# A hybrid layer on one core: who adds, gates and scales in the last round

## The chip, the core and the metric

The kernel runs on one core of one Trainium2 chip. The metric is the device time of one execution in microseconds (us). Before the change it is 2850.22 us, the median of 3 runs (2848.17 to 2852.48).

## What is computed

One layer of a hybrid network over a sequence of 2048 tokens of width 1024: a modulated norm, retention in both directions, grouped attention with a context of 256 tokens, an output projection, and then the part that matters here:

```python
x = x + g1 * (jnp.concatenate([ret, att], axis=-1) @ w_out)
h2 = _modulate(_rmsnorm(x, norm2_g), sh2, sc2)
x = x + g2 * _sqrelu_mlp(h2, w_ff1, w_ff2)      # square(relu(h2 @ w_ff1)) @ w_ff2, 4096 wide
...
return _rmsnorm(x, final_norm_g)                # x * rsqrt(mean(x*x) + eps) * g
```

The change concerns the last two lines: the residual sum with the gate `g2`, and the final norm, for the last of four slices of the hidden width.

## The kernel before

Products of the feed-forward part are made in split float16 (each float32 operand as a high and a low half, three matmuls for one product), and by a scheme with seven block products in place of eight. The second matmul is done in four rounds over the hidden width (`rd` 0 to 3). In a round the sixteen token tiles of 128 are taken in eight pairs, `PAIRS`, so there are 32 pairs in all, numbered 0 to 31; pairs 24 to 31 are the last round. A pair holds two token tiles, `g` = 0 and 1, and each tile has two halves of 512 columns, `n` = 0 and 1.

For each pair TensorE makes seven products (`down`, L1996 to L1998, 84 matmuls). `down_out` drains product `i` from PSUM: product 0 is copied by ScalarE (L2013), the others are added by VectorE to what was known (L2008). Four of these results are finished blocks and go to `gate`:

- after product 1 the block (`g` 0, `n` 0), after product 4 (1, 0), after product 5 (1, 1), after product 6 (0, 1);
- each is multiplied by the gate row `g2` (L2036) and added to the residual tile `y` (L2038);
- in the rounds before the last one the tile is stored to scratch; in the last round ScalarE squares each half and sums it (L2048), VectorE adds the two sums (L2056), GpSimd makes the root of the mean in two small ops (L1280, L1281), and VectorE multiplies the tile by the root and by the norm's weight in one op (L2063), after which it is stored.

GpSimd also makes the operands of the pair after (`sum_u`, L1981, four sums of 128x512 a pair); ScalarE rounds them to float16 (`hi_u`, L1985), and VectorE makes the remainder (`lo_u`, L1989, seven a pair).

Before the change all multiplications with the gate are on GpSimd, the sums for the halves `n` = 0 on GpSimd, and those for the halves `n` = 1 on VectorE. In the last pair both ops for the halves `n` = 1 are on VectorE.

The order on every engine is written out by hand: `on(at, phase, fn)` puts a call into a numbered step and a phase of it. Step by step, and in a step phase by phase, the calls are made in this order, and each engine runs its instructions in the order in which they were issued:

```python
FPHASES = ("pe", "sum", "hi", "lo", "relu", "out", "square", "late", "dma")
...
s = NU + 7 * p
...
on(s - 7, "sum", sum_u, p, "s1", "a21", "a22", ALU.add)
on(s - 6, "sum", sum_u, p, "s2", "s1", "a11", ALU.subtract)
on(s - 5, "sum", sum_u, p, "s3", "a11", "a21", ALU.subtract, "a21")
on(s - 3, "sum", sum_u, p, "s4", "a12", "s2", ALU.subtract, "s2")
```

So pair `p` begins at step `s`; a step is one product; the operand sums of a pair fall into the steps of the pair before. All transfers are issued from SyncE's queue (SP).

Of the kernel before, what the change touches and what calls it, by code (L numbers as in the profile page):

```python
# [11 lines left out]
F32 = mybir.dt.float32  # L12
F32R = mybir.dt.float32r
F16 = mybir.dt.float16
BF16 = mybir.dt.bfloat16
I32 = mybir.dt.int32
AF = mybir.ActivationFunctionType
ALU = mybir.AluOpType
# [4 lines left out]
P = 128  # L23
D = 1024
# [31 lines left out]
def layer_kernel(ctx: ExitStack, tc: tile.TileContext, a: dict, out: bass.AP):  # L56
    nc = tc.nc
# [27 lines left out]
    def scratch(name, n, shape, dtype=F32):  # L85
        return [dram.tile(shape, dtype, name=f"{name}{i}", tag=f"{name}{i}") for i in range(n)]
# [13 lines left out]
    x1_d = scratch("x1", NT, [P, D])  # L100
# [162 lines left out]
    with ExitStack() as st, tc.manual_schedule():  # L263
# [5 lines left out]
        op = st.enter_context(tc.tile_pool(name="op", bufs=2, reuse_waits="tile"))  # L269
        sm = st.enter_context(tc.tile_pool(name="sm", bufs=3, reuse_waits="tile"))  # L270
# [162 lines left out]
        class Rows:  # L433
# [11 lines left out]
            def square(self, n):  # L445
                if n % self.k == 0:
                    self.ss = sm.tile([P, self.k], F32, name="ss", tag=f"ss{self.k}", bufs=2)
                junk = tp.tile([P, D], BF16, name="junk", tag="junk", bufs=1)
                m = n % self.k
                nc.scalar.activation(junk, self.x[n], AF.Square, accum_out=self.ss[:, m : m + 1])  # L450
# [63 lines left out]
        g2 = one.tile([P, 2, 2, HD], F32, name="g2")  # L514
# [511 lines left out]
        for (g, c), w in weights.items():  # L1026
            if (g, c) > (0, 0):
                s = first[g, w.col]
# [5 lines left out]
        for g in (1, 2):  # L1034
            rows = Rows(GROUPS[g], 3)
            s = first[g - 1, C_RV]
# [33 lines left out]
        def slots(*what):  # L1070
            return [first[g, col] + n for g, col, ns in what for n in ns]

        two = (0, 0, 1, 1, 2, 2, 3, 3, 4, 4, 5, 5)
        at = slots((0, C_RQ, range(4)), (0, C_RV, two), (1, C_AQ, (1, 2, 3, 4)), (1, C_RK, (0, 0, 1, 2, 2, 3, 4, 4, 5)))
# [6 lines left out]
        at = slots((0, C_AKV, range(1, 6)), (0, C_AQ, range(4)), (0, C_RQ, range(4)), (1, C_AQ, range(6)))  # L1081
# [8 lines left out]
        s = first[2, C_RG]  # L1090
# [3 lines left out]
        for i in range(NK):  # L1094
            at = min(s + i + 1, len(units) - 1)
# [102 lines left out]
        for s, (g, c, m) in enumerate(units):  # L1198
# [3 lines left out]
            ps = psO.tile([P, 512], F32, name="pso", tag="pso")  # L1202
# [7 lines left out]
        s = len(units)  # L1210
# [9 lines left out]
    def pool(stack, name, bufs=1, **kw):  # L1220
        return stack.enter_context(tc.tile_pool(name=name, bufs=bufs, reuse_waits="tile", **kw))

    qp = pool(attn, "qp")
    op = pool(attn, "op2", 2)
# [4 lines left out]
    sm = pool(side, "sm2", 3, side="right")  # L1229
# [29 lines left out]
    def on(k, phase, fn, *args):  # L1259
        events.setdefault((k, phase), []).append((fn, args))  # L1260
# [16 lines left out]
    def rsqrt_chain(src, n, scale, tag, chain=chain, eps=EPS):  # L1277

        v, y = (sm.tile([P, n], F32, name=f"c{x}_{tag}", tag=f"c{x}_{tag}") for x in "vy")
        chain.append(lambda: nc.gpsimd.tensor_scalar(v, src, scale, eps, op0=ALU.mult, op1=ALU.add))  # L1280
        chain.append(lambda: nc.gpsimd.tensor_tensor(y, v, half[:, :n], op=ALU.pow))  # L1281
        return y
# [198 lines left out]
    def output_weights(k0):  # L1481
# [26 lines left out]
        for i in range(2 * KT):  # L1508
            k, n = i % KT, i // KT
            j = k0 + 4 + 4 * i  # L1510
            if i % 2 == 0:
                on(k0 + 1 if i == 0 else j - 5, "dma", fetch, k, n)
            on(j, "late", gate, k, n)
            on(j + 1, "late", part, k, n, 0)
            on(j + 2, "late", part, k, n, 1)
# [166 lines left out]
    ff = {}  # L1682
# [270 lines left out]
    PAIRS = [(rd, hf, q) for rd in range(4) for hf in range(2) for q in range(4)]  # L1953
    NAMES = ("a11", "a12", "a21", "a22")
    FORMS2 = ("a11", "a12", "s2", "s3", "a22", "s1", "s4")
    w2, uf, raw2, ys = {}, {}, {}, {}
# [14 lines left out]
    def tiles_of(p):  # L1971
        _, hf, q = PAIRS[p]
        return halves[hf][q], halves[hf][q + 4]
# [26 lines left out]
    xs_ = {}  # L2000

    def down_out(at, p, i):

        ps = pu.pop(i)

        def add(x, to=None):
            to = to if to is not None else ff["r"].tile([P, 512], F32, "d")
            nc.vector.tensor_tensor(to, ps, xs_[x], op=ALU.add)  # L2008
            return to

        if i == 0:
            xs_["x"] = ff["r"].tile([P, 512], F32, "d")
            nc.scalar.activation(xs_["x"], ps, AF.Copy)  # L2013
        elif i == 1:
            gate(at, p, 0, 0, add("x"))
        elif i == 2:
            xs_["u2"] = add("x")
        elif i == 3:
            xs_["u3"] = add("u2")
        elif i == 4:  # L2020
            gate(at, p, 1, 0, add("u3"))
        elif i == 5:
            gate(at, p, 1, 1, add("u3", xs_["u3"]))
            add("u2", xs_["u2"])
        elif i == 6:
            gate(at, p, 0, 1, add("u2", xs_["u2"]))

    sums = {}

    def gate(at, p, g, n, c):  # L2030
        s = slice(n * 512, (n + 1) * 512)
        y = ys[p, g][:, s]
        final = PAIRS[p][0] == 3
        fast = p == len(PAIRS) - 1 and n == 1
        eng = nc.vector if fast else nc.gpsimd
        on(at + 1, "square", lambda: eng.tensor_tensor(c, c, ff["g2"][:, s], op=ALU.mult))  # L2036
        eng2 = nc.vector if n or fast else nc.gpsimd
        on(at + 2, "lo" if eng2 is nc.vector else "square", lambda: eng2.tensor_tensor(y, y, c, op=ALU.add))  # L2038
        if not final:
            if n == 1:  # L2040
                on(at + 4, "dma", lambda: nc.sync.dma_start(x1_d[tiles_of(p)[g]], ys.pop((p, g))))
            return

        def square():
            if n == 0:
                sums[p, g] = ff["sm"].tile([P, 2], F32, name="ss", tag=f"ss{g}")
            junk = ff["sm"].tile([P, 512], BF16, name="junk", tag="junk", bufs=1)
            nc.scalar.activation(junk, y, AF.Square, accum_out=sums[p, g][:, n : n + 1])  # L2048

        on(at + 3, "relu", square)  # L2050
        if n == 1:
            on(at + 4, "lo", ending, at + 4, p, g)

    def ending(at, p, g):
        ss, y, t = sums.pop((p, g)), ys.pop((p, g)), tiles_of(p)[g]
        nc.vector.tensor_tensor(ss[:, :1], ss[:, :1], ss[:, 1:], op=ALU.add)  # L2056
        steps = []
        r = rsqrt_chain(ss[:, :1], 1, 1.0 / D, "e", steps)
        for step in steps:
            on(at, "square", step)  # L2060

        def whole(c):
            nc.vector.scalar_tensor_tensor(y[:, c], y[:, c], r, ff["fg"][:, c], op0=ALU.mult, op1=ALU.mult)  # L2063

        def store(c):
            nc.sync.dma_start(out[0, t * P : (t + 1) * P, c], y[:, c])

        n = 2 if p == len(PAIRS) - 1 else 1
        for i in range(n):
            c = slice(i * D // n, (i + 1) * D // n)  # L2070
            on(at + 1, "lo", whole, c)
            on(at + 1 if n == 2 else at + 3, "dma" if n == 1 else "lo", store, c)

    def down_jobs():
        for i in range(7):
            on(NU + 1 + i // 2, "dma", fetch_w2, 1, i)
        for p, (rd, hf, q) in enumerate(PAIRS):
            s = NU + 7 * p
            for m, blk in enumerate((2, 3, 0, 1)):
                on(s - 11 + m // 2, "dma", fetch_u, p, blk)  # L2080
            for g in range(2):
                on(s - 3 + g, "dma", fetch_y, p, g)
# [4 lines that stand above are left out]
            for i in range(7):  # L2087
                on(s - 7 + i, "hi", hi_u, p, i)
                on(s - 6 + i, "lo", lo_u, p, i)
                on(s + i, "pe", down, p, i)  # L2090
                on(s + i, "out", down_out, s + i, p, i)
                if (hf, q) == (1, 3) and rd in (0, 1):
                    on(s + i + 1, "dma", fetch_w2, rd + 2, i)
# [79 lines left out]
```

## Time and profile before

| what | value |
|---|---|
| median of 3 runs | 2850.22 us (2848.17 to 2852.48) |
| profiled execution | 2851.53 us |
| its span, first to last instruction | 2849.7 us |
| mean granted TensorE clock | 0.984 |
| TensorE busy | 2675.7 us, 94% of the span |
| VectorE busy | 2184.7 us, 77% |
| GpSimd busy | 1932.0 us, 68% |
| ScalarE busy | 1466.6 us, 51% |
| last matmul begins | at 2829.26 us |

How to read the lines that follow. A row of the timeline has the start from the beginning of the span and the duration, both in us, then the engine (PE is TensorE, DVE VectorE, ACT ScalarE, POOL GpSimd, SP SyncE), the line of the kernel, the operation, output and inputs by the program's names, the shapes, and how many instructions were merged into the row. In brackets stands how long the engine sat idle before it, and what ended the wait. A duration contains the time for which an instruction had been started but was held up, so it can be longer than the work. `pd` is a product in PSUM, `d` a block on its way to the residual, `y` a residual tile, `g2b` the gate row, `ss` the sums of squares, `cv_e` and `cy_e` the steps of the root, `fgb` the weight of the final norm, `ur` and `us` operands and their sums, `uf` their float16 halves.

### The profile page before, as it was taken

How to read it: one execution, taken by the hardware profiler on the slowest of the kernel's cores; microseconds unless marked ns; L12 is line 12 of the kernel's file. 1: busy time of each engine (PE TensorE's matmuls, PEld its weight loads, DVE VectorE, ACT ScalarE, POOL GpSimd, SP SyncE). 2: the span in 40 equal slices, each digit the busy share in tenths (PEclk: the TensorE clock that was granted, in tenths of full speed). 3: DMA queues.
4: the chain of work that ended last, by engine and by line, in shares of the span. 5: the costliest groups of instructions: out<-in, count | busy, mean ns of one | idle time of the engine just before them, and what ended most of it. 6: DMA issues, size and time to landing. Idle time of an engine off the chain costs nothing.

```text
span 2849.7 us, 46102 instructions
## 1 busy us (share of the span) xinstructions
PE 2675.7 (94%) x16756; PEld 1602.6 (56%) x16756; DVE 2184.7 (77%) x3122; ACT 1466.6 (51%) x2443; POOL 1932.0 (68%) x1499
## 2 busy tenths in 40 slices
PE   6899999898789999899999989999999999999996
PEld 3778688676556666566666634444444444444443
DVE  3587847778988777777778549788886688888898
ACT  2443443334677777777777735555554322222232
POOL 2436517434766667887667659888875688888887
PEclk8999999999999999999999989999999999999998
DMA  6684975565511212444112354677784757575643
GB/s 211 217 301 158 313 262 165 176 217 169 190 32 62 87 51 71 119 113 112 51 62 69 143 179 145 191 244 244 246 277 129 256 174 273 172 276 170 196 141 111
DMA packets 330467, 482.82 MB, mean 169 GB/s; under 512 B 82807, under 2 KB 193655, under 8 KB 325758
## 3 DMA queue, kind: packets, MB, share of 16 engines
q1 hardware_dynamic: 329854, 479.60, 51.2%
q8 instruction: 132, 2.16, 0.3%
q14 instruction: 97, 0.79, 0.1%
q10 hardware_dynamic: 384, 0.26, 0.0%
HBM read 327.57 MB, written 152.20 MB: 168 GB/s over the span
## 4 chain that ended last, share of the span: by engine, by line
PE 56%; DVE 8%; POOL 5%; issue 3%; DMA 2%; ACT 1%; SPq 0%; POOLq 0%; DVEq 0%; ACTq 0%
PE pu L1780 7%; PE pu L1779 7%; PE pu L1781 7%; PE pd L1998 5%; PE pd L1996 5%; PE pd L1997 5%; PE o L239 3%; PE st L205 3%; PE st L206 3%; PE mp L168 2%; PE bank L1545 2%; PE bank L1546 2%; DVE plo L224 2%; DVE nm L181 2%; PE bank L1547 2%
## 5 line engine op out<-in xcount | busy, mean ns | idle before, releaser
L181 DVE TENSOR_REDUCE nm<-mp 128x1 f32<-128x512 f32 (+1 forms) x576 | 390.5, 684 | 165.9 <-PE mp L168 136.9
L222 POOL TENSOR_TENSOR plo<-p,phi 128x1024 f16<-128x1024 f32 x160 | 352.5, 2204 | 165.2 <-ACT phi L215 133.2
L211 ACT ACTIVATE p<-st 128x512 f32<-128x512 f32 x576 | 338.3, 597 | 201.0 <-PE st L206 117.8
L1779 PE MATMUL pu<-hf,w1f 128*128 128x512 f16 x896 | 340.9, 380 | 0.0
L1780 PE MATMUL pu<-hf,w1f 128*128 128x512 f16 x896 | 340.9, 380 | 0.0
L1998 PE MATMUL pd<-w,uf 128*128 128x512 f16 x896 | 339.6, 379 | 1.3 <-DVE uf L1989 1.2
L1781 PE MATMUL pu<-hf,w1f 128*128 128x512 f16 x896 | 340.7, 380 | 0.0
L1996 PE MATMUL pd<-w,uf 128*128 128x512 f16 x896 | 339.6, 379 | 0.0
L1997 PE MATMUL pd<-w,uf 128*128 128x512 f16 x896 | 339.6, 379 | 0.0
L215 ACT ACTIVATE phi<-p 128x1024 f16<-128x1024 f32 x288 | 303.9, 1055 | 0.0
L1012 PE MATMUL pso<-whi,hhi_l 128*128 128x512 f32 (+1 forms) x768 | 298.8, 389 | 0.7 <-ACT whi L508 0.7
L1014 PE MATMUL pso<-whi,hlo_l 128*128 128x512 f32 (+1 forms) x768 | 289.2, 377 | 10.3 <-DVE hlo_l L488 10.3
L1013 PE MATMUL pso<-wlo,hhi_l 128*128 128x512 f32 (+1 forms) x768 | 288.2, 375 | 1.4 <-DVE wlo L512 1.4
L238 PE MATMUL o<-wv,plo 128*128 128x65 f16 x2304 | 234.8, 193 | 27.3 <-POOL plo L222 18.1
L224 DVE TENSOR_TENSOR plo<-p,phi 128x512 f16<-128x512 f32 x256 | 244.3, 955 | 16.8 <-ACT phi L215 16.2
L2036 POOL TENSOR_TENSOR d<-d,g2b 128x512 f32<-128x512 f32 x126 | 199.8, 1586 | 68.6 <-DVE d L2008 65.6
L239 PE MATMUL o<-wv,phi 128*128 128x129 f16 x2304 | 242.6, 220 | 0.0
L238 PEld LDWEIGHTS <-plo 128*128 128x128 f16 x2304 | 205.7, 98 | 64.0 <-POOL plo L222 28.0
L1791 DVE TENSOR_TENSOR r<-pu,r 128x512 f32<-128x512 f32 x224 | 151.0, 686 | 114.5 <-PE pu L1781 96.0
L1796 POOL TENSOR_TENSOR r<-r 128x512 f32<-128x512 f32 x128 | 168.6, 1322 | 94.5 <-ACT r L1795 93.9
L205 PE MATMUL st<-qr,ks 128*128 128x512 f16 x576 | 219.3, 381 | 11.7 <-ACT p L211 9.9
L206 PE MATMUL st<-qr,ks 128*128 128x512 f16 x576 | 219.5, 381 | 0.1
(324 smaller groups left out, 6290.2 us busy)
## 6 DMA issues: line engine op xcount, KB each, us to landing
wm<-in_w_ff SPq DMA_DIRECT2D x64, 512.0 KB, 6.7
u<-r SPq DMA_DIRECT2D x128, 256.0 KB, 4.6
ur<-u SPq DMA_DIRECT2D x128, 256.0 KB, 4.9
y<-x SPq DMA_DIRECT2D x64, 512.0 KB, 6.2
wst<-in_w_in SPq DMA_DIRECT2D x60, 512.0 KB, 6.2
wf<-w2f SPq DMA_DIRECT2D x112, 256.0 KB, 3.7
w<-wf SPq DMA_DIRECT2D x28, 1024.0 KB, 8.7
w1r<-in_w_ff SPq DMA_DIRECT2D x48, 512.0 KB, 5.0
```

Of the source, the lines that this page charges most:

```text
L181: nc.vector.tensor_reduce(dst, src, axis=AX.X, op=ALU.max, negate=True)
L206: mm(ps, ks2[:, self.g, k], q[:, 1], start=False, stop=True)
L211: nc.scalar.activation(self.p[kt // 2][:, kt % 2], self.s.pop(kt), AF.Exp, scale=HD**-0.5)
L222: nc.gpsimd.tensor_tensor(lo, p, hi, op=ALU.subtract)
L238: mm(o[:, : HD + 1], lo[:, i, c], v[:, : HD + 1], start=False, stop=False)
L239: mm(o, hi[:, i, c], v[:, :VW], start=False, stop=last)
L1779: mm(pu[hf, i], whi, hi, start=k == 0, stop=False)
L1780: mm(pu[hf, i], whi, lo, start=False, stop=False)
L1781: mm(pu[hf, i], wlo, hi, start=False, stop=k == 3)
L1996: mm(ps, u[:, 0, b], w[:, b, 0], start=b == 0, stop=False)
L1997: mm(ps, u[:, 0, b], w[:, b, 1], start=False, stop=False)
L1998: mm(ps, u[:, 1, b], w[:, b, 0], start=False, stop=b == 3)
```

## The change

In the last round the sum for the half (`g` 0, `n` 1) moves from VectorE to GpSimd, in pairs 24 to 30; VectorE keeps that for (1, 1). In the last but one pair, 30, the final scaling of both tiles is done in two ops, on ScalarE (times the root) and on GpSimd (times the norm's weight), in place of one on VectorE. In the last pair, 31, the half `n` = 1 of each tile is gated in two parts: what is known before the last product is multiplied by the gate and added to the residual tile first (for tile 1 on GpSimd, for tile 0 on VectorE), and the last product itself is then multiplied by the gate straight from PSUM and added by VectorE.

```diff
         elif i == 4:
             gate(at, p, 1, 0, add("u3"))
+            if p == len(PAIRS) - 1:
+                on(at, "square", direct, p, 1, xs_["u3"], nc.gpsimd)
+        elif i == 5 and p == len(PAIRS) - 1:
+            direct(p, 1, ps, nc.vector)
+            add("u2", xs_["u2"])
+            direct(p, 0, xs_["u2"], nc.vector)
+            squares(at + 2, p, 1, 1)
+        elif i == 6 and p == len(PAIRS) - 1:
+            direct(p, 0, ps, nc.vector)
+            squares(at + 1, p, 0, 1)
...
+    def direct(p, g, src, eng):
+        y, t = ys[p, g][:, 512:], ff["r"].tile([P, 512], F32, "d")
+        eng.tensor_tensor(t, src, ff["g2"][:, 512:], op=ALU.mult)
+        eng.tensor_tensor(y, y, t, op=ALU.add)
+
+    def squares(at, p, g, n):
+        y = ys[p, g][:, n * 512 : (n + 1) * 512]
+
+        def square():
+            if (p, g) not in sums:
+                sums[p, g] = ff["sm"].tile([P, 2], F32, name="ss", tag=f"ss{g}")
+            junk = ff["sm"].tile([P, 512], BF16, name="junk", tag="junk", bufs=1)
+            nc.scalar.activation(junk, y, AF.Square, accum_out=sums[p, g][:, n : n + 1])
+
+        on(at, "relu", square)
+        if n == 1:
+            on(at + 1, "lo", ending, at + 1, p, g)
...
     def gate(at, p, g, n, c):
         s = slice(n * 512, (n + 1) * 512)
         y = ys[p, g][:, s]
         final = PAIRS[p][0] == 3
-        fast = p == len(PAIRS) - 1 and n == 1
-        eng = nc.vector if fast else nc.gpsimd
-        on(at + 1, "square", lambda: eng.tensor_tensor(c, c, ff["g2"][:, s], op=ALU.mult))
-        eng2 = nc.vector if n or fast else nc.gpsimd
-        on(at + 2, "lo" if eng2 is nc.vector else "square", lambda: eng2.tensor_tensor(y, y, c, op=ALU.add))
...
+        on(at + 1, "square", lambda: nc.gpsimd.tensor_tensor(c, c, ff["g2"][:, s], op=ALU.mult))
+        eng = nc.vector if n and (g or not final) else nc.gpsimd
+        on(at + 2, "lo" if eng is nc.vector else "square", lambda: eng.tensor_tensor(y, y, c, op=ALU.add))
+        if final:
+            squares(at + 3, p, g, n)
+        elif n == 1:
+            on(at + 4, "dma", lambda: nc.sync.dma_start(x1_d[tiles_of(p)[g]], ys.pop((p, g))))
...
     def ending(at, p, g):
...
+        def scaled():
+            nc.scalar.activation(y, y, AF.Copy, scale=r)
+
+        def weighted():
+            nc.gpsimd.tensor_tensor(y, y, ff["fg"], op=ALU.mult)
+
+        if p == len(PAIRS) - 2:
+            on(at + 1, "relu", scaled)
+            on(at + 1, "square", weighted)
+            on(at + 2, "dma", store, slice(0, D))
+            return
         n = 2 if p == len(PAIRS) - 1 else 1
```

More of the change, by code (lines that the diff above doesn't have):

```diff
@@ L2033, in gate @@
         final = PAIRS[p][0] == 3
-        fast = p == len(PAIRS) - 1 and n == 1
-        eng = nc.vector if fast else nc.gpsimd
-        on(at + 1, "square", lambda: eng.tensor_tensor(c, c, ff["g2"][:, s], op=ALU.mult))
-        eng2 = nc.vector if n or fast else nc.gpsimd
[L2038 to L2052, printed above, removed]
+        on(at + 1, "square", lambda: nc.gpsimd.tensor_tensor(c, c, ff["g2"][:, s], op=ALU.mult))
[5 more added lines that the diff above has]
+            on(at + 4, "dma", lambda: nc.sync.dma_start(x1_d[tiles_of(p)[g]], ys.pop((p, g))))
     def ending(at, p, g):
```

## The prediction, made before the changed kernel ran

> **What bounds the kernel now.** I began with the span and the chain of waits, went on to the timeline of ScalarE through the last round to get the pace of the pairs, then to one pair on GpSimd (POOL) and VectorE (DVE), and last to the twenty microseconds behind the last matmul.
>
> ```profile
> span 2849.7 us, 46102 instructions
> ```
> ```profile
> 2685.43 0.60 ACT L2013 ACTIVATE d<-pd 128x512 f32<-128x512 f32 x1 [4.55 <-PE pd L1998]
> 2703.56 0.60 ACT L2013 ACTIVATE d<-pd 128x512 f32<-128x512 f32 x1 [3.25 <-PE pd L1998]
> 2722.13 0.58 ACT L2013 ACTIVATE d<-pd 128x512 f32<-128x512 f32 x1
> ...
> 2825.66 0.58 ACT L2013 ACTIVATE d<-pd 128x512 f32<-128x512 f32 x1
> ```
>
> L2013 runs once in a pair and drains the pair's first product. Up to 2703.56 it waits for TensorE and comes every 18.13 us: that is TensorE's own pace. Then the wait is gone and the pairs come every 20.71 us (2722.13 to 2825.66 is 103.53, in five steps). So in the last round, whose pairs also carry the final norm, TensorE runs ahead and something slower sets the pace. One such pair on POOL, and DVE's part of it:
>
> ```profile
> 2800.85 1.65 POOL L2036 TENSOR_TENSOR d<-d,g2b 128x512 f32<-128x512 f32 x1 [1.76 <-DVE d L2008]
> 2802.58 1.72 POOL L2038 TENSOR_TENSOR y<-y,d 128x512 f32<-128x512 f32 x1
> 2804.26 1.72 POOL L2036 TENSOR_TENSOR d<-d,g2b 128x512 f32<-128x512 f32 x1
> 2805.94 1.26 POOL L1981 TENSOR_TENSOR us<-ur 128x512 f32<-128x512 f32 x1
> 2807.16 1.72 POOL L2036 TENSOR_TENSOR d<-d,g2b 128x512 f32<-128x512 f32 x1
> 2808.84 1.71 POOL L1981 TENSOR_TENSOR us<-us,ur 128x512 f32<-128x512 f32 x1
> 2810.51 1.71 POOL L1981 TENSOR_TENSOR ur<-ur 128x512 f32<-128x512 f32 x1
> 2812.20 1.72 POOL L2036 TENSOR_TENSOR d<-d,g2b 128x512 f32<-128x512 f32 x1
> 2814.01 0.19 POOL L1280 TENSOR_SCALAR cv_e<-ss 128x1 f32<-128x1 f32 x1
> ...
> 2818.11 1.67 POOL L1981 TENSOR_TENSOR us<-ur,us 128x512 f32<-128x512 f32 x1
> 2821.55 1.65 POOL L2036 TENSOR_TENSOR d<-d,g2b 128x512 f32<-128x512 f32 x1 [1.76 <-DVE d L2008]
> ```
> ```profile
> 2806.01 1.74 DVE L2038 TENSOR_TENSOR y<-y,d 128x512 f32<-128x512 f32 x1 [1.16 <-POOL d L2036]
> 2807.67 1.75 DVE L1989 TENSOR_TENSOR uf<-ur,uf 128x512 f16<-128x512 f32 x1
> 2809.35 1.75 DVE L2038 TENSOR_TENSOR y<-y,d 128x512 f32<-128x512 f32 x1
> 2811.02 0.68 DVE L2008 TENSOR_TENSOR d<-pd,d 128x512 f32<-128x512 f32 x1
> ...
> 2818.59 2.28 DVE L2063 SCALAR_TENSOR_TENSOR y<-y,cy_e,fgb 128x1024 f32<-128x1024 f32 x1
> ```
>
> Two things are to be seen. First, the two engines take turns. POOL's op at 2805.94 ends at 2807.20; DVE's add, begun at 2806.01, ends 0.55 us after that; POOL's next op, begun at 2807.16, takes 1.72. Left alone a POOL op advances its queue by 1.22 (2805.94 to 2807.16); with one DVE op between, by 1.68 (2807.16 to 2808.84). So a DVE op on two SBUF operands takes 0.46 of POOL's time, and a POOL op 1.22 of DVE's. DVE ops that read a product from PSUM (L2008) keep to 0.68 throughout. Second, POOL's 1.76 of idle time is a link of a loop, not slack. POOL runs without a break from 2800.85 to 2819.78; DVE's L2063, begun at 2818.59, gets through only after that (to 2820.87); the drain L2008 behind it feeds POOL's next product with the gate at 2821.55. The loop is POOL's run of 18.93 plus 1.77 for L2063 and the drain: 20.70, the pace of the pairs. A longer run means a slower pair.
>
> Now the end, behind the last matmul:
>
> ```profile
> 2829.26 0.38 PE L1998 MATMUL pd<-w,uf 128*128 128x512 f16 x1
> ```
> ```profile
> 2824.95 2.95 POOL L2036 TENSOR_TENSOR d<-d,g2b 128x512 f32<-128x512 f32 x2
> 2829.73 1.26 POOL L2036 TENSOR_TENSOR d<-d,g2b 128x512 f32<-128x512 f32 x1 [1.83 <-DVE ss L2056]
> 2831.08 0.19 POOL L1280 TENSOR_SCALAR cv_e<-ss 128x1 f32<-128x1 f32 x1
> 2831.35 0.55 POOL L1281 TENSOR_TENSOR cy_e<-cv_e,half 128x1 f32<-128x1 f32 x1
> ...
> 2836.89 1.27 POOL L2036 TENSOR_TENSOR d<-d,g2b 128x512 f32<-128x512 f32 x1 [2.00 <-DVE d L2008]
> ```
> ```profile
> 2826.70 2.35 DVE L2038 TENSOR_TENSOR y<-y,d 128x512 f32<-128x512 f32 x2 [1.16 <-POOL d L2036]
> ...
> 2831.94 2.27 DVE L2063 SCALAR_TENSOR_TENSOR y<-y,cy_e,fgb 128x1024 f32<-128x1024 f32 x1 [0.93 <-POOL cy_e L1281]
> ...
> 2834.93 1.28 DVE L2063 SCALAR_TENSOR_TENSOR y<-y,cy_e,fgb 128x1024 f32<-128x1024 f32 x1
> ...
> 2841.41 0.69 DVE L2038 TENSOR_TENSOR y<-y,d 128x512 f32<-128x512 f32 x1
> ```
>
> TensorE is done at 2829.64, and 20.06 us of elementwise work and stores remain. The last residual sum starts at 2841.41; from there to the end of the span (squares, root, scaling, stores of the last tile) are 8.29 us.
>
> **The change, part by part.** *The moved sum.* In pairs 24 to 30 the second half of the first tile's residual sum (DVE at 2809.35) goes to POOL; the built order puts it there between the operand sums that stood at 2808.84 and 2810.51. From 2804.26 to 2814.01 POOL now has six full ops, with five DVE turns between them: 6 x 1.22 + 5 x 0.46 = 9.62, and the rows say 9.75. Afterwards it has seven ops and four turns: 7 x 1.22 + 4 x 0.46 = 10.38. The run grows by 0.76 per pair. On DVE 1.67 goes (2809.35 to 2811.02), but DVE's queue waits for POOL at L2063 anyway. The square behind the moved sum comes later on ScalarE, and ahead of the two operand copies queued there; those wait for POOL's operand sum at 2810.51 in any case, so that costs nothing; without that cover it would be one square, 0.6. The bounds are 0 (the idle 1.76 is slack after all) and 1.22 a pair (DVE's freed turn is filled by another op of its own). I take 0.76, which is what the turns give. The loop sets the pace for the five steps from 2722.13; the first I count half, since ScalarE still waited 3.25 for TensorE at 2703.56: 4.5 x 0.76 = 3.4.
>
> *Pair 30 scaled elsewhere.* Two DVE ops (L2063, 2.27 and 1.28) become, for each tile, one ScalarE op on 128x1024 with the root as scale and one POOL product with the norm weight on 128x1024. The rows nearest:
>
> ```profile
> L215 ACT ACTIVATE phi<-p 128x1024 f16<-128x1024 f32 x288 | 303.9, 1055 | 0.0
> ```
> ```profile
> L222 POOL TENSOR_TENSOR plo<-p,phi x160: 2118/2132/2695, 674.1 to 1619.9; 128x1024 f16<-128x1024 f32 x160
> ```
>
> ScalarE: 1.06. POOL: two 128x512 advances make 2.44; below stands the median 2.13 of L222, whose output has half the bytes, above its 2.69 under contention. I take 2.44. [...] No row here has this form.
>
> *The last pair.* Its gate products and sums for the second halves are split: what is known goes first (on POOL for one tile, on DVE for the other), the last product is gated straight from PSUM. For the tile on POOL these two ops stand in the queue behind both 2.44 products, and DVE's sum of the same half waits for them. On the old clock, without the 3.4:
>
> - POOL ends the two gate products at 2827.90 and takes the moved sum behind DVE's one remaining sum (2828.36): 2829.6. The gate product of 2829.73 comes when it did, ends at 2830.8; root for one tile (2831.08 and 2831.35 above, 0.82 in all) to 2831.7; the sum, 1.22, to 2832.95. ScalarE scales meanwhile, to 2832.8.
> - First 2.44 product: 2835.4. Second root, 0.82: 2836.2. ScalarE's scaling, 1.06 and about 0.1 of handing over, with POOL standing behind it: 2837.4. Second product: 2839.85.
> - Only now the known part of the last pair: product and sum, 2 x 1.22: 2842.3. Before the change POOL's gate product of the last pair had begun at 2836.89.
> - POOL goes straight on with the other tile half's gate product, so DVE's sum gets in at 2843.5 and ends at 2844.1. POOL's sum follows to 2845.3 while DVE drains from PSUM (0.6); DVE's product with the gate gets in at 2845.3, to 2845.8; sum 0.6, product from PSUM 0.6; last sum at 2847.0.
>
> The last sum starts at 2847.0 instead of 2841.41: 5.6 later, with the same 8.29 behind it. If DVE wins the turn at 2842.3, its later ops lose theirs and the last sum comes at 2846.8. With 2.13 for the products it is 5.0, with 2.69 it is 6.1. The pair's two stores leave on SP behind POOL instead of DVE, at 2835.4 and 2839.85; with ten microseconds left they hide.
>
> *Sum:* 3.4 + 5.6 = 9.0. The profiled execution took 2851.53 (1.83 around its span), so it would take 2860.5; it stands 1.31 above the median of 2850.22, so the forecast is 2859.2.
>
> **The turns, once more.** The rows at 2805.94 to 2811.02 show an op that waits out the other's whole op. [...]
>
> **Rivals.**
> - *Only the tail* (0.10): the loop has slack, since DVE, a sum shorter, reaches L2063 earlier. 5.6, so 2855.8. Against it: L2063 already ends at POOL's release at 2819.78, not at its own start.
> - *Every freed turn is used* (0.09): 4.5 x 1.22 + 6.1 = 11.6, so 2861.8. For it: DVE has seven operand remainders (L1989) per pair, several undelayed now.
> - *DVE is the bound* (0.05), the other side: the idle 1.76 is true slack, and DVE's queue sets the pair. Then each pair loses DVE's 1.67, 4.5 x 1.67 = 7.5, and the tail loses the two L2063, 3.55: 2839.2. It decides from the point where POOL's added 1.22 fits into 1.76 without moving L2063. DVE's 1.16 wait for POOL at 2806.01 speaks against it.
> - *The late sums hide* (0.05): if the two 2.44 products don't hold up the last pair, only the 3.4 stays: 2853.6. It needs the last pair's sums to stand ahead of them in POOL's queue, and the built order has them behind.
>
> **Numbers.** The forecast, 2859.2, has 0.71 and a range of its own from 2856.5 to 2862. About 0.2%, 5.7 us, is what a measurement of this kernel can tell from no change. Slower by more: forecast, used turns, and half of the tail alone, 0.85. Same: the other half and the hidden sums, 0.10. Faster: 0.05. The range from 2854.5 to 2863 takes the bounds of the prices (5.0 with no loss in the loop, 6.1 with 1.22 a pair, and 1 of scatter at the top) and leaves out the DVE rival and the hidden sums.
>
> **What would show it.** Steps of 21.4 to 21.5 between L2013's rows from the second step on, and still an idle of about 1.8 before one gate product a pair, would show the loop; steps of 20.7 or less refute it. Two POOL products of 2.1 to 2.7 behind L2013's last row, POOL without a gap of over 1.3 up to the last pair's known sum, and DVE waiting for that sum by some 5 us would show the tail. Last matmul to end of span should grow from 20.1 to about 25.7. The forecast is wrong if DVE reaches its last residual sum as early behind the last L2013 as before, 15.75.

## The result, and the profile after

| | before | changed |
|---|---|---|
| median of 8 runs | 2849.51 us (2844.77 to 2853.1) | 2859.68 us (2854.62 to 2865.27) |
| ratio | 1 | 1.0038, 95% interval 1.0026 to 1.0049 |
| span of the profiled execution | 2849.7 us | 2861.6 us |
| step: from one pair's drain on ScalarE (L2013) to the next, last five | 20.71 us | 21.61 us |
| tail: from the last of these drains to the end of the span | 24.04 us | 29.83 us |
| from the last drain to the last residual sum on VectorE | 15.75 us | 21.52 us |

The changed kernel is 10.2 us slower by the medians; by the interval of the ratio the difference lies between 7.4 and 14 us. The forecast was 2859.2.

ScalarE's drains in the changed kernel, from its timeline (start, duration, in brackets the wait):

```profile
span 2861.6 us, 46105 instructions
```
```profile
2687.00 0.60 ACT L2013 ACTIVATE d<-pd 128x512 f32<-128x512 f32 x1 [4.55 <-PE pd L1998]
2705.13 0.60 ACT L2013 ACTIVATE d<-pd 128x512 f32<-128x512 f32 x1 [3.24 <-PE pd L1998]
2723.72 0.58 ACT L2013 ACTIVATE d<-pd 128x512 f32<-128x512 f32 x1
2745.33 0.58 ACT L2013 ACTIVATE d<-pd 128x512 f32<-128x512 f32 x1
...
2831.77 0.58 ACT L2013 ACTIVATE d<-pd 128x512 f32<-128x512 f32 x1
```

Up to the drain with the 3.24 wait nothing differs but a shift of 1.57 (2705.13 against 2703.56). It is there already at the first drain of the last round (2687.00 against 2685.43), ahead of every changed instruction. In the traces of all kernels of this document the drain that is at 2705.13 here comes between 2696.4 and 2705.1, so the shift is taken for scatter from one execution to the next; where it comes from is not shown. From that drain to the last are 126.64 us, against 122.10 before: 4.54 more. With the tail's 5.79 the change costs 10.33 in the traces; the medians say 10.17. In what follows step and tail are compared, not single times.

One pair on GpSimd, and two rows of VectorE from the same stretch:

```profile
2809.45 1.72 POOL L2062 TENSOR_TENSOR d<-d,g2b 128x512 f32<-128x512 f32 x1
2811.14 1.26 POOL L1981 TENSOR_TENSOR us<-ur 128x512 f32<-128x512 f32 x1
2812.36 1.72 POOL L2062 TENSOR_TENSOR d<-d,g2b 128x512 f32<-128x512 f32 x1
2814.04 1.72 POOL L1981 TENSOR_TENSOR us<-us,ur 128x512 f32<-128x512 f32 x1
2815.72 1.71 POOL L2064 TENSOR_TENSOR y<-y,d 128x512 f32<-128x512 f32 x1
2817.40 1.27 POOL L1981 TENSOR_TENSOR ur<-ur 128x512 f32<-128x512 f32 x1
2818.62 1.72 POOL L2062 TENSOR_TENSOR d<-d,g2b 128x512 f32<-128x512 f32 x1
2820.43 0.19 POOL L1280 TENSOR_SCALAR cv_e<-ss 128x1 f32<-128x1 f32 x1
...
2827.65 1.65 POOL L2062 TENSOR_TENSOR d<-d,g2b 128x512 f32<-128x512 f32 x1 [1.76 <-DVE d L2008]
```
```profile
2817.98 1.24 DVE L1989 TENSOR_TENSOR uf<-us,uf 128x512 f16<-128x512 f32 x1
...
2824.69 2.28 DVE L2079 SCALAR_TENSOR_TENSOR y<-y,cy_e,fgb 128x1024 f32<-128x1024 f32 x1
```

The moved sum stands at 2815.72. The idle time ahead of the pair's gate product is 1.76, the same as before, with one more op in the run before it: it was a link of the loop, not slack. The end of the kernel, on GpSimd, on VectorE and, for the scaling of pair 30 by the root, on ScalarE:

```profile
2839.08 2.34 POOL L2088 TENSOR_TENSOR y<-y,fgb 128x1024 f32<-128x1024 f32 x1
...
2843.59 2.34 POOL L2088 TENSOR_TENSOR y<-y,fgb 128x1024 f32<-128x1024 f32 x1 [1.26 <-ACT y L2085]
2845.89 1.26 POOL L2042 TENSOR_TENSOR d<-d,g2b 128x512 f32<-128x512 f32 x1
2847.23 1.26 POOL L2043 TENSOR_TENSOR y<-y,d 128x512 f32<-128x512 f32 x1
2848.45 1.26 POOL L2062 TENSOR_TENSOR d<-d,g2b 128x512 f32<-128x512 f32 x1
```
```profile
2838.25 0.68 DVE L2042 TENSOR_TENSOR d<-pd,g2b 128x512 f32<-128x512 f32 x1
2848.52 1.73 DVE L2043 TENSOR_TENSOR y<-y,d 128x512 f32<-128x512 f32 x1 [9.60 <-POOL y L2043]
...
2853.29 0.69 DVE L2043 TENSOR_TENSOR y<-y,d 128x512 f32<-128x512 f32 x1
```
```profile
2842.37 1.15 ACT L2085 ACTIVATE y<-y,cy_e 128x1024 f32<-128x1024 f32 x1 [2.55 <-POOL cy_e L1281]
```

GpSimd works through the two wide products of pair 30 (128x1024, L2088) first; ScalarE's scaling (L2085) stands between them. VectorE has gated the last product of its half from PSUM at 2838.25 and then stands still for 9.60, until GpSimd has added the known part of the same half. VectorE gets its sum through only behind GpSimd's next product (2848.45 to 2849.71): the sum lasts 1.73, against 0.69 for the one at 2853.29, and ends 0.54 behind that product.

### The profile page after: what moved, and what is told of

It is laid out like the page before. It is cut to its first block, busy times and chain, and to the rows that moved or that the text cites. A ratio compares the mean times of both kernels' runs of the same rounds, so it can differ in the third digit from the quotient of the medians.

```text
span 2861.6 us, 46105 instructions
## 1 busy us (share of the span) xinstructions
PE 2683.2 (94%) x16756; PEld 1607.5 (56%) x16756; DVE 2180.3 (76%) x3113; ACT 1470.6 (51%) x2445; POOL 1945.4 (68%) x1510
## 4 chain that ended last, share of the span: by engine, by line
PE 50%; POOL 11%; DVE 7%; issue 4%; DMA 1%; ACT 1%; SPq 0%; POOLq 0%; DVEq 0%; ACTq 0%
PE pu L1780 7%; PE pu L1779 7%; PE pu L1781 7%; PE pd L1998 3%; PE pd L1997 3%; PE pd L1996 3%; PE o L239 3%; PE st L205 3%; PE st L206 3%; POOL d L2062 3%; PE mp L168 2%; POOL us L1981 2%; DVE nm L181 2%; PE bank L1545 2%; PE bank L1547 2%
```

## The experiments

Every experiment is read by step and tail from one profiled execution. A step is the mean over the last five steps between drains, in e7 to e10 over the steps that are alike (in e10 the last one, 18.56, is left out). The last column is the start of VectorE's last residual sum. The single times of e1 to e8 are not used, because those of one and the same kernel scatter by several us: e2 took 2850.13 us, 0.74 less than the one execution of the kernel before that ran beside it, where about 4.5 more was expected, and e1 took 3.75 more where about 5.8 was expected.

| kernel | step | tail | last sum on VectorE, behind the last drain |
|---|---|---|---|
| before | 20.71 | 24.04 | 15.75 |
| changed | 21.61 | 29.83 | 21.52 |
| e1: changed, moved sum back | 20.71 | 29.99 | 21.71 |
| e2: moved sum alone | 21.61 | 23.83 | 15.56 |
| e3: changed, scaling back | 21.61 | 25.65 | 17.31 |
| e4: changed, wide products last | 21.60 | 27.40 | 17.61 |
| e5: scaling alone | 20.71 | 26.94 | 11.77 |
| e6: last pair alone | 20.71 | 25.87 | 17.51 |
| e7: sum left out | 20.25 | 23.53 | 15.19 |
| e8: one more GpSimd op | 21.93 | 25.13 | 16.83 |
| e9: the other way | 19.70 | 22.41 | 14.06 |
| e10: further | 19.63 | 22.48 | 14.12 |

### e1 and e2: the moved sum, taken back and alone

```diff
-        eng = nc.vector if n and (g or not final) else nc.gpsimd
+        eng = nc.vector if n else nc.gpsimd
```

> The changed kernel with the moved sum alone put back on VectorE in pairs 24 to 30; the scaling of pair 30 and the last pair stay changed. Measured: the step between ScalarE's drains (20.71 before, 21.61 changed) and the tail from the last of these drains to the end of the span (24.04 before, 29.83 changed). Theory (loop and tail are separate): steps of 20.7, tail 29.5 to 30.1, so about 5.8 over the time before. Rival (the tail is long because GpSimd arrives there late): steps of 20.7 and a tail under 28.

The drains and the span of e1:

```profile
span 2852.8 us, 46106 instructions
```
```profile
2719.27 0.58 ACT L2013 ACTIVATE d<-pd 128x512 f32<-128x512 f32 x1
...
2822.81 0.58 ACT L2013 ACTIVATE d<-pd 128x512 f32<-128x512 f32 x1
```

103.54 in five steps, 20.71, and a tail of 29.99: the theory's numbers. The opposite kernel is the one before with this edit:

```diff
-        eng2 = nc.vector if n or fast else nc.gpsimd
+        eng2 = nc.vector if fast or (n and (g or not final)) else nc.gpsimd
```

> The kernel before with the moved sum alone. Theory: steps of 21.6, tail 23.7 to 24.3, about 4.5 over the time before. Rival (moved sum and scaling together make the step long): steps under 21.2.

The span and the drains of e2:

```profile
span 2848.3 us, 46102 instructions
```
```profile
2716.42 0.58 ACT L2013 ACTIVATE d<-pd 128x512 f32<-128x512 f32 x1
...
2824.47 0.58 ACT L2013 ACTIVATE d<-pd 128x512 f32<-128x512 f32 x1
```

e2 has the step of the changed kernel (108.05 in five steps, 21.61) and, within 0.2, the tail of the kernel before (23.83 against 24.04). So loop and tail are separate, and the loop's part is wholly the moved sum's.

### e3, e5 and e6: the two parts of the tail

e3 sends pair 30 through the old scaling, in `ending`:

```diff
-        if p == len(PAIRS) - 2:
+        if False:
```

> The changed kernel with the scaling of pair 30 put back on VectorE; moved sum and last pair stay. Theory (the two wide GpSimd products hold up the last pair): steps 21.6, tail 25 to 26.5. Rival (the new form of the last pair is the cost): tail over 28.

The tail falls from 29.83 to 25.65, as the theory said. The other two kernels are the one before with the new scaling of pair 30 alone (e5), and the changed kernel without the scaling and without the moved sum (e6, the edits of e1 and e3 together). The edit of e5:

```diff
+        def scaled():
+            nc.scalar.activation(y, y, AF.Copy, scale=r)
+
+        def weighted():
+            nc.gpsimd.tensor_tensor(y, y, ff["fg"], op=ALU.mult)
+
+        if p == len(PAIRS) - 2:
+            on(at + 1, "relu", scaled)
+            on(at + 1, "square", weighted)
+            on(at + 2, "dma", store, slice(0, D))
+            return
```

> The kernel before with the scaling of pair 30 on ScalarE and GpSimd alone. Theory: steps 20.7; the two wide products stand ahead of the gate product of half (1, 0) of the last pair on GpSimd; tail 26.5 to 27.5. Rival (only the known sums queued on GpSimd suffer): tail under 25.

> The kernel before with the new form of the last pair alone. Theory: two more ops on GpSimd and one more turn for VectorE, nothing gained, since what sets the end is the number of ops behind the last drain: steps 20.7, tail 25.5 to 26.5. Rival (gating the known part ahead shortens the end by itself): tail under 24.

e5 adds 2.90 to the tail, e6 1.83. Together, in e1, they add 5.95, which is 1.2 more than their sum. It fits that only together the known product and sum of the last pair stand behind the wide products on GpSimd; this share was not tried by itself. e5 shows that the products hurt without that:

```profile
2828.04 1.26 POOL L2036 TENSOR_TENSOR d<-d,g2b 128x512 f32<-128x512 f32 x1 [1.84 <-DVE ss L2056]
...
2831.47 2.35 POOL L2072 TENSOR_TENSOR y<-y,fgb 128x1024 f32<-128x1024 f32 x1
...
2836.76 2.34 POOL L2072 TENSOR_TENSOR y<-y,fgb 128x1024 f32<-128x1024 f32 x1 [1.26 <-ACT y L2069]
2839.05 1.26 POOL L2036 TENSOR_TENSOR d<-d,g2b 128x512 f32<-128x512 f32 x1
2840.39 1.26 POOL L2038 TENSOR_TENSOR y<-y,d 128x512 f32<-128x512 f32 x1
2843.45 0.19 POOL L1280 TENSOR_SCALAR cv_e<-ss 128x1 f32<-128x1 f32 x1 [1.79 <-DVE ss L2056]
```

The gate product of the last pair's half (1, 0) starts at 2839.05, 15.09 behind the last drain (2823.96); before the change this was 11.23. VectorE, freed of its two scalings, starts its last sum after 11.77 instead of 15.75, and wins nothing: the end now waits for GpSimd's sum at 2840.39. And e6 shows that the new form of the last pair is itself a loss, 1.83 us, in the place where it was to be ahead of the work.

### e4: the wide products issued last

```diff
-            on(at + 1, "square", weighted)
-            on(at + 2, "dma", store, slice(0, D))
+            on(NU + 7 * p + 13, "late", weighted)
+            on(NU + 7 * p + 13, "dma", store, slice(0, D))
```

> The changed kernel with the same work, but the two wide GpSimd products of pair 30 issued behind GpSimd's gate products and sums of the last pair. Theory with place and turns: the known sum no longer waits, but VectorE's last sums each wait out a wide product: tail 26.5 to 27.7, between before and changed. Rival (place alone is the cost): tail under 25. Rival (place is nothing): tail stays at 29.8.

27.40: between the two. The end on GpSimd and on VectorE:

```profile
2839.94 5.54 POOL L2088 TENSOR_TENSOR y<-y,fgb 128x1024 f32<-128x1024 f32 x2
```
```profile
2837.12 1.73 DVE L2043 TENSOR_TENSOR y<-y,d 128x512 f32<-128x512 f32 x1 [3.66 <-POOL y L2043]
...
2840.56 2.72 DVE L2043 TENSOR_TENSOR y<-y,d 128x512 f32<-128x512 f32 x1
2843.20 0.68 DVE L2042 TENSOR_TENSOR d<-pd,g2b 128x512 f32<-128x512 f32 x1
2843.91 2.12 DVE L2043 TENSOR_TENSOR y<-y,d 128x512 f32<-128x512 f32 x1
```

VectorE's wait for the known sum falls from 9.60 to 3.66: that was the place in the queue. But now two of its last sums, 0.69 in the changed kernel, take 2.72 and 2.12 beside the two wide products (2839.94 to 2845.48), and the second ends 0.55 behind them; the product from PSUM between the sums keeps its 0.68. In the first place the wide products cost by standing ahead, in the second by their turns. Only these two places behind the last drain were tried; whether there is one that costs nothing is not shown.

### e7 and e8: the price of a turn and of an op

e7 leaves the sum of half (0, 1) out on both engines; e8 keeps it on VectorE and adds a GpSimd op where the moved sum would stand (its output is bfloat16, the moved sum's is float32).

```diff
+        if not (final and not fast and (g, n) == (0, 1)):
             on(at + 2, "lo" if eng2 is nc.vector else "square", lambda: eng2.tensor_tensor(y, y, c, op=ALU.add))
```
```diff
+        if final and not fast and (g, n) == (0, 1):
+            def more():
+                x = ff["sm"].tile([P, 512], BF16, name="more", tag="more", bufs=1)
+                nc.gpsimd.tensor_tensor(x, c, ff["g2"][:, s], op=ALU.add)
+            on(at + 2, "square", more)
```

> The kernel before, leaving out the residual sum of half (0, 1) in pairs 24 to 30 on either engine. It prices the sum's turn on VectorE. If the freed turn goes (the prediction): steps of 20.2, 0.46 less than before. If the next op takes the freed turn: steps of 20.7. If VectorE's whole op counts: steps of 19.0.

> The kernel before with one more GpSimd op of 128x512 where the moved sum would stand, its result unused, and the sum still on VectorE. It prices a GpSimd op without taking a VectorE op away. Theory: the step grows by 1.2 to 1.3, to 21.9 or 22.0. If GpSimd's idle 1.76 is slack: 20.7. If the moved sum costs 0.9 whatever VectorE does: 21.6.

e7 steps by 20.25: 0.46 less, the price of a turn. e8 steps by 21.93: 1.22 more, the price of a GpSimd op. Both stand in the prediction to the hundredth. In both kernels the idle time before the pair's first gate product is still 1.76. But the changed kernel, which has the added op and lacks the turn, does not step by 20.71 + 1.22 - 0.46 = 21.47; it steps by 21.61. Where the missing 0.14 may lie is to be seen beside e7, GpSimd above and VectorE below:

```profile
2802.07 1.27 POOL L2036 TENSOR_TENSOR d<-d,g2b 128x512 f32<-128x512 f32 x1
2803.42 0.52 POOL L1280 TENSOR_SCALAR cv_e<-ss 128x1 f32<-128x1 f32 x1
```
```profile
2802.64 1.24 DVE L1989 TENSOR_TENSOR uf<-us,uf 128x512 f16<-128x512 f32 x1
```

In e7 the operand remainder L1989 gets its turn in front of a root op, which lasts 0.33 longer (0.52 for 0.19); e8 has the same. In the changed kernel the same remainder (2817.98) gets in ahead of a gate product (2818.62), which lasts 0.45 longer (1.72 for 1.27). In the kernel before it ran one place later, beside the root ops, and held up the sum behind them (1.45 there, 1.27 in the changed kernel at 2821.22):

```profile
2814.80 1.45 POOL L2038 TENSOR_TENSOR y<-y,d 128x512 f32<-128x512 f32 x1
```
```profile
2814.45 0.67 DVE L1989 TENSOR_TENSOR uf<-us,uf 128x512 f16<-128x512 f32 x1
```

The difference of 0.12 is close to the missing 0.14; that it is the whole cause was not tried by itself.

### e9 and e10: the other way

If GpSimd's run sets the step, work should go from it to VectorE.

```diff
-        eng = nc.vector if fast else nc.gpsimd
+        eng = nc.vector if fast or (final and (g, n) in [(0, 0)]) else nc.gpsimd
...
-        eng2 = nc.vector if n or fast else nc.gpsimd
+        eng2 = nc.vector if fast or (final and (g, n) in [(0, 0), (1, 1)]) or (not final and n) else nc.gpsimd
```

> The kernel before, with work of the last round moved the other way: the gate product and the sum of half (0, 0) go from GpSimd to VectorE, and the sum of half (0, 1) from VectorE to GpSimd. GpSimd has one op of 128x512 less a pair, VectorE one more. Theory (GpSimd's run sets the step): 1.22 less and a turn of 0.46 more, steps of 19.9 or, where the new turn falls into a gap, 19.5; tail about 24; 4 to 7 under the time before. Rival (VectorE is as much the bound): steps of 20.7 or more.

2837.89 us (2837.09 to 2839.65, 5 runs) against 2848.01 of the kernel before on the same chip (2842.02 to 2852.66, 12 runs): ratio 0.9962, interval 0.9949 to 0.9976. It is faster than the kernel before, and so than the changed one. Its drains:

```profile
2699.41 0.60 ACT L2013 ACTIVATE d<-pd 128x512 f32<-128x512 f32 x1 [3.25 <-PE pd L1998]
2717.54 0.60 ACT L2013 ACTIVATE d<-pd 128x512 f32<-128x512 f32 x1 [0.56 <-PE pd L1998]
2736.58 0.58 ACT L2013 ACTIVATE d<-pd 128x512 f32<-128x512 f32 x1
...
2815.39 0.57 ACT L2013 ACTIVATE d<-pd 128x512 f32<-128x512 f32 x1
```

The step is 19.70, and TensorE still sets the pace one pair longer (the wait of 0.56). From the first of these drains to the last it is 115.98 against 122.10, and the tail is 1.63 shorter: 7.75 in all by the traces, more than the 4 to 7 expected. The tail of about 24 that was expected did not come; it is 22.41. The edit also moves the two ops of half (0, 0) in the last pair, but why the tail is shorter was not tried. The medians' 10.1 is not set against that: single times of the kernel before alone lie over 10 us apart.

The gain per pair is not GpSimd's whole gain:

```profile
2791.57 1.65 POOL L2036 TENSOR_TENSOR d<-d,g2b 128x512 f32<-128x512 f32 x1 [2.42 <-DVE d L2008]
...
2807.60 1.26 POOL L1981 TENSOR_TENSOR us<-ur,us 128x512 f32<-128x512 f32 x1
```

GpSimd's run is 17.29 now (2791.57 to 2808.86), 1.64 shorter than the 18.93 before, but the idle time in front of it is 2.42 instead of 1.76, so the step is only 1.01 shorter. What VectorE still has to do behind the last op of GpSimd's run has grown by the rest: its drain, which the next gate product waits for, ends 2.35 behind that op (2811.21 against 2808.86), and 1.69 behind it before (2821.47 against 2819.78).

e10 goes on: the gate products of (0, 0) and (0, 1) and the sum of (1, 0) on VectorE, the sum of (0, 1) on GpSimd.

```diff
+        eng = nc.vector if fast or (final and (g, n) in [(0, 0), (0, 1)]) else nc.gpsimd
...
+        eng2 = nc.vector if fast or (final and (g, n) in [(1, 0), (1, 1)]) or (not final and n) else nc.gpsimd
```

> The kernel before with more of the same: the gate products of the halves (0, 0) and (0, 1) on VectorE, the sum of (1, 0) on VectorE and that of (0, 1) on GpSimd. GpSimd has two ops less a pair. Theory: twice the step's gain, steps of 18.6 to 19.2, until TensorE's 18.13 ends it; 5 to 9 under the time before. Rival (VectorE becomes the bound): steps longer than those of the run with one op less.

The theory's step did not come. 2839.5 us (2836.35 to 2845.9, 8 runs), ratio 0.9971, interval 0.9961 to 0.9981; the step is 19.63, hardly shorter than with one op less. On GpSimd there are now gaps:

```profile
2798.21 1.66 POOL L2038 TENSOR_TENSOR y<-y,d 128x512 f32<-128x512 f32 x1 [1.83 <-DVE d L2036]
...
2802.84 1.65 POOL L2038 TENSOR_TENSOR y<-y,d 128x512 f32<-128x512 f32 x1 [0.36 <-DVE d L2036]
```

GpSimd waits 1.83 and 0.36 for gate products that are now VectorE's. Here the rival is the nearer one: the waits show VectorE's queue as a second link of the loop, if not to the point of a longer step.

## Why the prediction was right

**The loop.** That GpSimd's run, with VectorE's scaling and drain behind it, sets the pace: right, shown by the idle of 1.76 that stays the same in the changed kernel, e7 and e8, by the step of 21.61 in e2, and from the other side by e9. Two things in this term were off. The step grew by 0.90 where 0.76 was taken, and so came out as 21.61 instead of 21.4 to 21.5: the prices of op and turn were right, each by itself (e8 and e7), but the sum counted the freed turn as gone, and another op of VectorE took it. And the first of the five steps was counted half, for the wait of 3.25 one drain ahead of it; it came out whole (2723.72 to 2745.33 is 21.61). So the term was 4.54 instead of 3.4.

**The tail.** Right in mechanism and size: 5.6 forecast, 5.77 measured to the last sum, and 8.31 behind it where 8.29 was taken. By its own points, behind the last drain: the first wide product starts after 7.31 (forecast 7.29), the second ends after 14.16 (14.19), the known sum ends after 16.72 (16.64), the last sum starts after 21.52 (21.34). A wide product took 2.34 where 2.44 was taken, ScalarE's scaling 1.15 instead of 1.06; that these errors nearly cancel is luck. One sign was missed: VectorE was to wait for the known sum by some 5 us and waited 9.60. It came to the wait earlier than was thought, 7.16 behind the last drain; since the sum it waits for was timed rightly, the end did not move.

**The rivals.** "Only the tail" and "VectorE is the bound" fall with the step of 21.61 in e2. "The late sums hide" falls with VectorE's wait of 9.60 and with e3. "Every freed turn is used" describes the long part of GpSimd's run rightly: in the changed kernel the seven GpSimd ops from 2809.45 to the first root op at 2820.43 take 10.98, 1.23 more than the six before (2804.26 to 2814.01, 9.75). That is a whole op of 1.22, so the freed turn was refilled there. From that root op to the next pair's first gate product, the idle time included, it is 7.22 against 7.54; the 0.32 that comes back there leaves the 0.9.

**The sum.** 9.0 was forecast, 10.33 is in the traces, 10.17 in the medians. That the time itself, 2859.2, is within 0.5 of the measured 2859.68 is partly luck: the median of the kernel before came out 0.71 lower in 8 runs than in the 3 that the forecast started from, and that hides 0.7 of the 1.2 by which the sum fell short of the medians.

## What to carry to other kernels

An idle stretch on an engine is not room for work when what ends it depends on that engine's own last instruction (here 1.76 before the change and 1.76 after it): follow the idle back one turn of the loop before filling it. Where two engines take turns, as here at 0.46 and 1.22 a turn, price a moved op by the other's turns as well, and look at which op will take the freed turn. And of work that can wait, ask whose queue it stands in at the end: the two products nobody waited for, with the scaling between them, cost 2.9 us by themselves (e5) and more with a sum queued behind them.

## What was not expected

VectorE's two scalings of pair 30, 3.55 us of its time, could be taken away in the tail without any gain (e5: its last sum came 4 us earlier, the end 2.9 later). And a change of the opposite direction, one op of 128x512 off GpSimd and one more on VectorE, took 7.75 us off by the traces, in a kernel in which VectorE was the busier of the two (77% of the span against 68%).
